# Mixing products of two transformer layers: three token tiles summed feature by feature instead of after all features

## The chip, the cores and the metric

The kernel runs on one core of a Trainium2 chip. The metric is device time in microseconds (us) of one execution, the median of three runs. Five engines are named: PE (TensorE, matrix products), DVE (VectorE), ACT (ScalarE), POOL (GpSimd) and SP (SyncE, which here issues the DMA transfers). PE writes its sums to PSUM, a memory of eight banks; one bank holds a 128x512 fp32 tile.

## What is computed

Two different transformer layers follow one another, for one sequence of T = 1024 tokens with a width of D = 1024, in fp32. The part that matters is the end of each layer's mixing stage and the step to its feed-forward part:

```python
# layer 1 (site A)
mix = jnp.concatenate([y_att, y_rwkv], axis=-1) @ w_out
x = x + g_m * rms_norm(mix, mix_post_norm)
hf = rms_norm(x, ffn_pre_norm) * (1 + sc_f) + sh_f      # then hf @ w_ffn_gate, hf @ w_ffn_up
...
# layer 2 (site B)
yb = ob @ w_b_out
mixed = jax.nn.sigmoid(gate_a) * ya + jax.nn.sigmoid(gate_b) * yb
h = h + _rmsnorm(mixed @ w_o, g_mix_post)
u2 = _rmsnorm(h, g_ffn_pre)                             # then u2 @ w_ffn_up
```

`mix` and `mixed @ w_o` are the two mixing products. Each is [1024 x 1024] times [1024 x 1024].

## The kernel before, in words

**Precision.** Every fp32 operand of these products is split into a high and a low part. One product of a pair is three matmuls (`mm3`, L101 to L107): high by high (L105), high by low (L106), low by high (L107). The split of a weight tile is an ACT copy for the high part and a subtraction on POOL or DVE for the low part (`rows_w`, L1397 and L1398); the split of a feature tile is the same in `Ops.put` (L237, L238).

**Tiles.** The tokens form 8 token tiles of 128, the 1024 features form 8 tiles k (called features below), each with its 128 rows of the weight matrix. `row_product` (L1403) computes one token tile: for each half of the 1024 output columns it sums all 8 features, 3 matmuls each, so 48 matmuls of 128x512 into one PSUM tile of two banks.

**Site A** (L1902 to L1948). The features come from DRAM: 4 to 7 first, then 0 to 3, each cast by ACT L237 and DVE L238. Weight 4 is loaded and cast early, into a free part of the feature store; the other seven are loaded on SP and cast after the last feature, in the order 5, 6, 7, 0, 1, 2, 3, the low parts shared between POOL and DVE. PSUM is laid out as two two-bank tiles `ps` for products and four one-bank tiles `tr` for transposes. Then the pipeline runs.

**The pipeline** (`pipeline`, L555, over the generator `mixed`, L1885) sends each token tile i through four steps, and in one round it issues a step each of several tiles, the newest tile first. The steps are: the product; then `stats` (ACT L534 squares and sums the PSUM tile, POOL L114 and L115 make the reciprocal root), `post_add` (DVE L542 reads the PSUM tile, DVE L543 adds the input x) and the store; then `stats` of the new x and `renorm` (DVE L549, at site A also L551); then, for two tiles together, `put_pair` (L247 to L284): eight 128x128 transposes per token tile on PE (L255) into two `tr` tiles, read by ACT (L260, L266, L272) and DVE (L261, L274 to L279), which write the operands of the feed-forward products. A `ps` tile comes free when DVE L542 has read it. Tiles `xt` and `xn` share a ring of four buffers, two token tiles' worth. Each engine works through its instructions in the order of issue.

**Site B** (L2026 to L2062). The features do not come from DRAM; each is made on PE. For m = 0 to 7, `fm` sums four inputs `ob` by `w_b_out_2` into a two-bank `ps` tile (ring of three): 24 matmuls of 128x512. DVE multiplies by a gate (L2052) and adds a tile `ma` loaded on SP (L2051, one buffer; DVE L2053); ACT L237 and DVE L238 split the result into feature m. The weights of the mixing product are loaded within the loop, m = 2 to 6, weights 0 and 1 before it and weight 7 after it, in the place of an input that `fm` no longer needs. Weight loads and `w_b_out_2` share the ring `wraw`. Then the same pipeline runs, with PSUM laid out anew as at A.

After each site the feed-forward part of the layer begins on PE (L291 to L293).

Of the kernel before, what the change touches and what calls it, by code (L numbers as in the profile page):

```python
# [19 lines left out]
D = 1024  # L20
NT = 8
# [173 lines left out]
def fm(c, w, kt, act, m0=0, m=128):  # L195

    return fms(c, [w], kt, act, m0, m)[0]


def fms(c, ws, kt, act, m0=0, m=128):  # L200

    act = Feat(act) if isinstance(act, list) else act
    ps = [c.psum([m, T]) for _ in ws]
    for hf in range(2):
        sl = slice(hf * 512, hf * 512 + 512)
        for p, w in zip(ps, ws):
            c.mm3(p[:, sl], [((w[:, 0, k, m0:m0 + m], w[:, 1, k, m0:m0 + m]), (act.cols(k, 0, hf), act.cols(k, 1, hf))) for k in range(kt)])
    return ps


def split(c, x, out_hl, eng=None):

    nc = c.nc
    nc.scalar.activation(out_hl[:, 0], x, AF.Copy)  # L214
    (eng or nc.gpsimd).tensor_sub(out_hl[:, 1], x, out_hl[:, 0].bitcast(FP))  # L215
# [315 lines left out]
def stats(c, x, junk):  # L531

    ss = c.small.tile([128, 1], FP, name="ss", tag="ssp", bufs=8)
    c.nc.scalar.activation(junk, x, AF.Square, scale=float(D) ** -0.5, accum_out=ss)  # L534
    r = c.rsqrt(ss, 1, 1.0, EPS)
    return r


def post_add(c, y, r, x, G, out, t):

    nc = c.nc
    nc.vector.scalar_tensor_tensor(t, y, r, G, op0=ALU.mult, op1=ALU.mult)  # L542
    nc.vector.tensor_add(out, t, x)  # L543


def renorm(c, t, x, r, g, b=None):

    nc = c.nc
    nc.vector.scalar_tensor_tensor(t, x, r, g, op0=ALU.mult, op1=ALU.mult)  # L549
    if b is not None:  # L550
        nc.vector.tensor_add(t, t, b)  # L551
    return t


def pipeline(gens):  # L555

    active, gens = [], iter(gens)
    more = True
    while more or active:
        g = next(gens, None)  # L560
        more = g is not None
        if more:
            active.insert(0, g)
        active = [g for g in active if next(g, active) is not active]
# [57 lines left out]
def load_rows_over(c, t, src, k, sl=slice(0, T)):  # L622

    for par in range(2):
        c.nc.sync.dma_start(t[64 * par:64 * par + 64], src[k, par, sl].partition_broadcast(64))
# [764 lines left out]
def rows_w(c, ap, w, ks, name="wo", bufs=None, at={}, eng=None):  # L1390

    nc = c.nc
    out = []
    for k in ks:
        raw = c.load_rows(w, k)
        hl = at[k] if k in at else ap.tile([128, 2, w.shape[1]], FR, name=name, bufs=bufs or len(ks) - len(at))
        nc.scalar.activation(hl[:, 0], raw, AF.Copy)  # L1397
        (eng or nc.gpsimd).tensor_sub(hl[:, 1], raw, hl[:, 0].bitcast(FP))  # L1398
        out.append(hl)
    return out  # L1400


def row_product(c, act, wt, i, ks=None):  # L1403

    ps = c.psum([128, D])
    for hf in range(2):
        sl = slice(hf * 512, hf * 512 + 512)
        c.mm3(ps[:, sl], [((act.tok(k, 0, i), act.tok(k, 1, i)), (wt[k][:, 0, sl], wt[k][:, 1, sl])) for k in ks or range(len(wt))])
    return ps
# [320 lines left out]
def row_bcast(c, ap, v, name):  # L1730

    t = ap.tile([128, D], FP, name=name)
    c.nc.sync.dma_start(t, v.partition_broadcast(128))
    return t
# [66 lines left out]
def two_layers(ctx, tc, *args):  # L1801
    out = args[-1]
    p = dict(zip(INS, args))
# [6 lines left out]
    c = Core(ctx, tc)  # L1810
    c.n8, c.n4 = 8, 6
    nc = c.nc
    pool = lambda n, side="left": tc.tile_pool(name=n, bufs=1, reuse_waits="tile", side=side)
    x1d, x2d, h1d = (tc.dram_tile([T, D], FP, name=n) for n in ("x1d", "x2d", "h1d"))
    cqd = tc.dram_tile([3, 128, 2 * T], FP, name="cqd")

    def loader(ap, src, tag="s4", bufs=None):
        def get(i):
            t = ap.tile([128, D], FP, name="xt", tag=tag, bufs=bufs or c.n4)
            nc.sync.dma_start(t, src[i * 128:(i + 1) * 128])  # L1820
            return t
        return get
# [57 lines left out]
    def store(dst, i, x):  # L1880
        nc.sync.dma_start(dst[i * 128:(i + 1) * 128], x)

    xns = [None] * NT

    def mixed(i, ap, h, wt, get, dst, G, g, b=None):  # L1885

        ps = row_product(c, h, wt, i)
        yield
        xt = get(i)
        xn = xns[i] = ap.tile([128, D], FP, name="xn", tag="s4", bufs=c.n4)  # L1890
        r = stats(c, ps, xn)
        post_add(c, ps, r, xt, G, xt, xn)
        store(dst, i, xt)
        yield
        r = stats(c, xt, xn)
        renorm(c, xn, xt, r, g, b)
        yield
        if i % 2:
            yield from h.put_pair(c, i // 2, xns[i - 1], xn)
# [5 lines left out]
    h = Ops(hp.__enter__(), "h")  # L1905
    c.layout(qk=(1, 3), tp=(1, 3), o=(1, 2))
    wt = [None] * 8
# [24 lines left out]
        features(3)  # L1932
        c.wlayout()
    at.__exit__(None, None, None)
    c.layout(ps=(2, 2), tr=(1, 4))
    wp = pool("wo1")
    wp1 = wp.__enter__()
    c.wlayout(3, 0)
    for n, k in enumerate((5, 6, 7, 0, 1, 2, 3)):
        wt[k] = rows_w(c, wp1, p["w_out"], [k], "wo", 7, eng=nc.vector if n % 3 else None)[0]  # L1940
    c.wlayout()
    c.n4 = 4
    with pool("mo2") as ap:
        g1s = h.t[:, 3, 6].rearrange("p k x t -> p (k x t)").bitcast(FP)
        nc.sync.dma_start(g1s, r1.partition_broadcast(128))
        Gh, Bh = (row_bcast(c, ap, v, n) for v, n in ((rg, "Gh"), (rb, "Bh")))
        c.tp, c.nt2 = ap, 4
        pipeline(mixed(i, ap, h, wt, loader(ap, x_in), x1d, g1s, Gh, Bh) for i in range(NT))  # L1948
    wp.__exit__(None, None, None)
    fd = tc.dram_tile([22, 128, T], FP, name="f_d")  # L1950
    c.layout(ps=(1, 8))
# [16 lines left out]
    with Down(c, pool, "d1") as dn:  # L1968
        get = loader(dn.ap, x1d)
        h = []  # L1970
# [20 lines left out]
    h = h[0]  # L1991
# [9 lines left out]
    with pool("pe") as ap:  # L2001
        pT = Tok(ap, "pT", 2)
        for i in range(NT):
            t = ap.tile([128, 256], FP, name="px", bufs=4)
            nc.sync.dma_start(t, p["p_2"][i * 128:(i + 1) * 128])
            pT.put_T(c, i, t)
        wt = rows_w(c, ap, p["w_ple_proj_2"], range(2))
        for i in range(NT):
            t = ap.tile([128, D], FP, name="et", bufs=2)
            nc.scalar.activation(t, row_product(c, pT, wt, i), AF.Copy)  # L2010
            store(ed, i, t)
# [11 lines left out]
    c.wlayout()  # L2023
    m0p.__exit__(None, None, None)
    c.wlayout(3, 4)
    c.layout(ps=(2, 3), tr=(1, 2))  # L2026
    hp = pool("hp2")
    h = Ops(hp.__enter__(), "h2")
    c.wlayout(2, 3)
# [2 lines left out]
    rows = lambda k: rows_w(c, woa, p["w_o_2"], [k], "woa", 7, eng=nc.vector if k % 2 else None)  # L2032
    wt = rows(0) + rows(1)
    with pool("mo3") as ap:
        ob = []
        for k in range(4):
            t = ap.tile([128, T], FP, name="yl", tag="ms", bufs=2)
            nc.sync.dma_start(t, obd[k])
            r = ap.tile([128, T], FP, name="yr", tag="ma", bufs=1)
            load_rows_over(c, r, b2.rd, k)  # L2040
            nc.vector.tensor_mul(t, t, r)
            y = h.free(k)
            split(c, t, y, nc.vector)
            ob.append(y)
        for m in range(8):
            ps = fm(c, c.split_w(c.load_cols(p["w_b_out_2"], m * 128, 128, 4)), 4, ob)
            if 2 <= m < 7:
                wt += rows(m)
            s, a = ap.tile([128, T], FP, name="ms", bufs=2), ap.tile([128, T], FP, name="ma", bufs=1)
            nc.sync.dma_start(s, b2.sgb[m])  # L2050
            nc.sync.dma_start(a, b2.mA[m])  # L2051
            nc.vector.tensor_mul(s, s, ps)  # L2052
            nc.vector.tensor_add(s, s, a)  # L2053
            h.put(c, m, s, nc.vector)
        wt += rows_w(c, ap, p["w_o_2"], [7], at={7: h.free(3)}, eng=nc.vector)
    c.wlayout()
    c.n4 = 4
    c.layout(ps=(2, 2), tr=(1, 4))
    with pool("mo4") as ap:
        G3, Gh = row_bcast(c, ap, p["g_mix_post_2"], "G3"), row_bcast(c, ap, p["g_ffn_pre_2"], "Gh2")  # L2060
        c.tp, c.nt2 = ap, 4
        pipeline(mixed(i, ap, h, wt, loader(ap, x2d), h1d, G3, Gh) for i in range(NT))  # L2062
    wp.__exit__(None, None, None)
    fd = tc.dram_tile([22, 128, T], FP, name="f2_d")
    c.layout(ps=(1, 8))
# [8 lines left out]
    with Down(c, pool, "d2") as dn:  # L2074
        get = loader(dn.ap, h1d)
        h = []
# [16 lines left out]
    h = h[0]  # L2093
# [5 lines left out]
    with pool("pl") as ap:  # L2099
        G5 = row_bcast(c, ap, p["g_ple_post_2"], "G5")  # L2100
        get, get_e = loader(ap, x1d), loader(ap, ed)
        wt = rows_w(c, ap, p["w_ple_gate_2"], range(8))
# [17 lines left out]
def make_kernel(fn, ins, outs, extra=None):  # L2120
    def kernel(**inputs):
# [18 lines left out]
        return got[0] if len(got)==1 else got  # L2140
    return kernel
kernel = make_kernel(two_layers, INS, [((1, 1024, 1024), "float32")], lambda: {"onehot": bucket_rows(), "inv_freq": inv_freq()})
```

## Time and profile before

| what | value |
|---|---|
| median of three runs | 3823.2 us (3817.89 to 3823.93) |
| profiled execution, its own time | 3827.49 us |
| its span, first to last instruction | 3825.8 us |
| mean granted clock of TensorE | 0.867 |
| PE busy | 3303.5 us, 86% of the span |
| DVE busy | 2363.7 us, 62% |
| ACT busy | 1422.0 us, 37% |
| POOL busy | 1086.0 us, 28% |

A row of the timeline is a start, a duration, the engine with its line and operation, the tiles out<-in, and in brackets how long the engine was idle before it and what released it. Times are us from the start of the span. PEclk is the granted clock of TensorE as a share of full speed. PE's matmuls overlap, so that two starts tell its pace and a single duration does not.

### The profile page before, as it was taken

The numbers are of one execution on the slowest core, as the hardware profiler recorded it, in microseconds if no ns is written. First come the engines' busy times: TensorE is split into PE (matmuls) and PEld (weight loads), VectorE is DVE, ScalarE is ACT, GpSimd is POOL, SyncE is SP. The second block draws the span as 40 slices with busy tenths as digits, with TensorE's granted clock in tenths as the row PEclk, the third lists the DMA queues.
The fourth block names the chain that finished last, engine by engine and source line by source line (L and its number), as shares of the span: only waits on it lengthen the run. The fifth ranks groups of instructions, "written<-read, shape, count | busy, mean of one in ns | idle before, by whom it ended". The sixth has DMA issues, their size and how long they took to land.

```text
span 3825.8 us, 42329 instructions
## 1 busy us (share of the span) xinstructions
PE 3303.5 (86%) x15652; PEld 2641.3 (69%) x15652; DVE 2363.7 (62%) x3607; ACT 1422.0 (37%) x2417; POOL 1086.0 (28%) x1007
## 2 busy tenths in 40 slices
PE   3788767998994879999897999989988799998988
PEld 2666545776773658887675888778866588886767
DVE  5569977657644365554998110016763688889983
ACT  3345433333333243333434111236642444444332
POOL 3114245424321022221444222131020122223432
PEclk7788765556566889999997999989989899999989
DMA  5462232211214122222333122210062222213234
GB/s 174 148 174 71 90 122 65 68 42 59 53 51 146 61 83 83 83 83 72 112 136 100 48 68 82 100 55 10 12 198 78 78 83 83 83 61 138 90 147 149
DMA packets 259200, 347.76 MB, mean 91 GB/s; under 512 B 17216, under 2 KB 194337, under 8 KB 257969
## 3 DMA queue, kind: packets, MB, share of 16 engines
q1 hardware_dynamic: 257936, 344.82, 27.6%
q8 instruction: 123, 2.02, 0.2%
q14 instruction: 85, 0.69, 0.1%
q0 software_dynamic: 1056, 0.23, 0.0%
HBM read 253.17 MB, written 91.83 MB: 90 GB/s over the span
## 4 chain that ended last, share of the span: by engine, by line
PE 60%; DVE 23%; DMA 7%; issue 4%; ACT 3%; POOL 2%; SPq 1%; DVEq 0%; POOLq 0%; ACTq 0%
PE ps L291 8%; PE ps L293 8%; PE ps L292 8%; PE ps L105 7%; PE ps L107 7%; PE ps L106 7%; DVE junk L845 3%; DVE sm L432 3%; DVE acc L464 2%; PE o L596 2%; DVE op L440 2%; PE tp L588 2%; DMA adaw<-in_ada_w_dram 1%; PE xy L1289 1%; DVE tmp L1225 1%
## 5 line engine op out<-in xcount | busy, mean ns | idle before, releaser
L291 PE MATMUL ps<-h,op 128*128 128x512 f32 x1232 | 481.1, 396 | 13.5 <-ACT op L314 11.6
L292 PE MATMUL ps<-h,op 128*128 128x512 f32 x1232 | 487.2, 395 | 0.0
L293 PE MATMUL ps<-h,op 128*128 128x512 f32 x1232 | 486.4, 396 | 0.0
L316 POOL TENSOR_TENSOR op<-t,op 128x512 fp32r<-128x512 f32 x88 | 129.5, 1471 | 647.8 <-ACT op L314 574.6
L291 PEld LDWEIGHTS ps<-h,op 128*128 128x128 f32 x1232 | 233.2, 189 | 69.3 <-ACT op L314 12.4
L291 PE MATMUL ps<-op,op 128*128 128x512 f32 x616 | 246.8, 403 | 34.3 <-DVE acc L464 19.7
L293 PEld LDWEIGHTS ps<-h,op 128*128 128x128 f32 x1232 | 232.7, 189 | 54.8 <-DVE op L316 0.6
L292 PEld LDWEIGHTS ps<-h,op 128*128 128x128 f32 x1232 | 232.9, 189 | 54.2
L293 PE MATMUL ps<-op,op 128*128 128x512 f32 x616 | 244.4, 397 | 6.6 <-DVE op L440 6.4
L292 PE MATMUL ps<-op,op 128*128 128x512 f32 x616 | 244.6, 397 | 6.0 <-POOL op L440 5.5
L89 POOL TENSOR_TENSOR whl<-wraw,whl 128x1024 fp32r<-128x1024 f32 (+1 forms) x62 | 130.2, 2102 | 392.2 <-ACT whl L88 363.4
L1710 DVE TENSOR_TENSOR up<-t,ps 128x512 f32<-128x512 f32 x176 | 116.6, 683 | 199.4 <-ACT t L354 153.7
L354 ACT ACTIVATE t<-ps 128x512 f32<-128x512 f32 x132 | 78.5, 595 | 384.1 <-PE ps L293 382.1
L105 PE MATMUL ps<-h,whl 128*128 128x512 f32 x512 | 205.8, 404 | 9.6 <-ACT h L214 7.9
L107 PE MATMUL ps<-h,whl 128*128 128x512 f32 x512 | 204.9, 400 | 1.2 <-POOL whl L89 1.2
L106 PE MATMUL ps<-h,whl 128*128 128x512 f32 x512 | 205.3, 401 | 0.3 <-DVE h L215 0.3
L464 DVE TENSOR_TENSOR acc<-acc,ps 128x1024 f32<-128x1024 f32 x152 | 180.1, 1208 | 10.1 <-PE ps L293 9.0
L596 PE MATMUL o<-pT,v 128*128 128x256 f32 (+1 forms) x640 | 157.9, 366 | 13.4 <-ACT pT L591 7.8
L291 PEld LDWEIGHTS ps<-op,op 128*128 128x128 f32 x616 | 117.5, 191 | 74.1 <-DVE acc L464 18.4
L591 ACT ACTIVATE pT<-tp 128x512 fp32r<-128x512 f32 (+2 forms) x221 | 94.6, 444 | 186.9 <-PE tp L588 149.4
L114 POOL TENSOR_SCALAR rs_y<-ss 128x1 f32<-128x1 f32 (+2 forms) x90 | 32.7, 364 | 457.0 <-ACT xn L534 283.0
L438 ACT ACTIVATE op<-sm 128x1024 fp32r<-128x1024 f32 (+1 forms) x96 | 94.5, 987 | 177.0 <-DVE sm L432 149.5
(589 smaller groups left out, 8342.7 us busy)
## 6 DMA issues: line engine op xcount, KB each, us to landing
wraw<-in_w_ffn_up_dram SPq DMA_DIRECT2D x66, 512.0 KB, 4.0
adaw<-in_ada_w_dram SPq DMA_DIRECT2D x96, 256.0 KB, 3.5
raw<-in_w_ffn_down_dram SPq DMA_DIRECT2D x44, 512.0 KB, 6.5
raw<-f_d SPq DMA_DIRECT2D x44, 512.0 KB, 5.3
wraw<-in_w_in_dram SPq DMA_DIRECT2D x42, 512.0 KB, 3.9
wraw<-in_w_ffn_gate_dram SPq DMA_DIRECT2D x22, 512.0 KB, 3.9
f_d<-up SPq DMA_DIRECT2D x22, 512.0 KB, 2.6
f_d<-cv SPq DMA_DIRECT2D x22, 512.0 KB, 2.6
```

What stands on the lines that cost most here:

```text
L89: self.nc.gpsimd.tensor_sub(hl[:, 1], raw, hl[:, 0].bitcast(FP))
L105: self.nc.tensor.matmul(out, lh, rh, start=first and i == 0, stop=False)
L106: self.nc.tensor.matmul(out, lh, rl, start=False, stop=False)
L107: self.nc.tensor.matmul(out, ll, rh, start=False, stop=last and i == n - 1)
L291: mm(out, lh, rh, start=start and i == 0, stop=False, skip_group_check=True)
L292: mm(out, lh, rl, start=False, stop=False, skip_group_check=True)
L293: mm(out, ll, rh, start=False, stop=stop and i == n - 1, skip_group_check=True)
L316: (nc.gpsimd if n[0] % 7 in (0, 3, 5) else nc.vector).tensor_sub(t[:, 1], x, t[:, 0].bitcast(FP))
L432: getattr(eng, what)(x, a, b)
L464: nc.vector.tensor_add(d, d, ps[q])
L596: nc.tensor.matmul(o[:, q], v[:, b0 + s].rearrange("p a d -> p (a d)"), pT[:, x, s, q], start=b0 == 0 and n == 0, stop=end and n == 3)
L1710: nc.vector.tensor_add(halves(x[j])[e], tok(a), tok(b))
```

## The change

There are three parts.

First, a new function `k_step` adds one feature's part to three PSUM tiles: 3 token tiles x 2 halves x 3 matmuls, so 18. It is called for each feature as soon as feature and weight are issued. The three PSUM tiles hold token tiles 0 to 2; their step of the product falls away from `mixed`, and these tiles enter the pipeline with their statistics. Tiles 3 to 7 are computed by `row_product` as before. PSUM is laid out for both as three two-bank tiles `po` and two one-bank tiles `tr`.

Second, at site A weight 4's step comes first, the low parts of the seven other weights all go to DVE, and each weight's step follows its cast.

Third, at site B a feature is made in two halves of 512 columns, each in a one-bank `tr` tile, since the two-bank tiles are taken; the gate is multiplied by half (two instructions in place of one). The step of feature m - 1 stands behind the making of feature m. The layout is not changed between the loop and the pipeline.

```diff
+def k_step(c, act, w, k, pss, first, last):
+
+    for i, ps in enumerate(pss):
+        for hf in range(2):
+            sl = slice(hf * 512, hf * 512 + 512)
+            c.mm3(ps[:, sl], [((act.tok(k, 0, i), act.tok(k, 1, i)), (w[:, 0, sl], w[:, 1, sl]))], first, last)
...
-def row_product(c, act, wt, i, ks=None):
+def row_product(c, act, wt, i, ks=None, tag="ps"):
-    ps = c.psum([128, D])
+    ps = c.psum([128, D], tag)
...
-    def mixed(i, ap, h, wt, get, dst, G, g, b=None):
-        ps = row_product(c, h, wt, i)
-        yield
+    def mixed(i, ap, h, wt, pss, get, dst, G, g, b=None):
+        if i < len(pss):
+            ps = pss[i]
+        else:
+            ps = row_product(c, h, wt, i, tag="po")
+            yield
...
-    c.layout(ps=(2, 2), tr=(1, 4))
+    c.layout(po=(2, 3), tr=(1, 2))
+    pss = [c.psum([128, D], "po") for _ in range(3)]
...
-    for n, k in enumerate((5, 6, 7, 0, 1, 2, 3)):
-        wt[k] = rows_w(c, wp1, p["w_out"], [k], "wo", 7, eng=nc.vector if n % 3 else None)[0]
+    for n, k in enumerate((4, 5, 6, 7, 0, 1, 2, 3)):
+        if n:
+            wt[k] = rows_w(c, wp1, p["w_out"], [k], "wo", 7, eng=nc.vector)[0]
+        k_step(c, h, wt[k], k, pss, n == 0, n == 7)
...
-    c.layout(ps=(2, 3), tr=(1, 2))
+    c.layout(po=(2, 3), tr=(1, 2))
...
+        pss = [c.psum([128, D], "po") for _ in range(3)]
         for m in range(8):
-            ps = fm(c, c.split_w(c.load_cols(p["w_b_out_2"], m * 128, 128, 4)), 4, ob)
-            if 2 <= m < 7:
-                wt += rows(m)
+            w = c.split_w(c.load_cols(p["w_b_out_2"], m * 128, 128, 4))
             s, a = ap.tile([128, T], FP, name="ms", bufs=2), ap.tile([128, T], FP, name="ma", bufs=1)
             nc.sync.dma_start(s, b2.sgb[m])
             nc.sync.dma_start(a, b2.mA[m])
-            nc.vector.tensor_mul(s, s, ps)
+            for hf in range(2):
+                sl = slice(hf * 512, hf * 512 + 512)
+                ps = c.psum([128, 512], "tr")
+                c.mm3(ps, [((w[:, 0, k], w[:, 1, k]), (ob[k][:, 0, sl], ob[k][:, 1, sl])) for k in range(4)])
+                nc.vector.tensor_mul(s[:, sl], s[:, sl], ps)
+            if 2 <= m < 7:
+                wt += rows(m)
+            if m:
+                k_step(c, h, wt[m - 1], m - 1, pss, m == 1, False)
             nc.vector.tensor_add(s, s, a)
             h.put(c, m, s, nc.vector)
         wt += rows_w(c, ap, p["w_o_2"], [7], at={7: h.free(3)}, eng=nc.vector)
+        k_step(c, h, wt[7], 7, pss, False, True)
...
-    c.layout(ps=(2, 2), tr=(1, 4))
```

The gate's multiplication is L2069 after the change (L2052 before), the addition of `ma` L2074 (L2053 before).

The order of the instructions moves with it. Three places follow.

The first is PE at the end of site A: the last matmuls of token tile 7's product, then transposes (L255), then the feed-forward part. Before:

```order
L106 MATMUL ps<-wo,h 128x512
L107 MATMUL ps<-wo,h 128x512
L105 MATMUL ps<-wo,h 128x512
L106 MATMUL ps<-wo,h 128x512
L107 MATMUL ps<-wo,h 128x512
L255 MATMUL tr<-ident,xn 128x128 x32
L291 MATMUL ps<-h,op 128x512
```

With the change:

```order
L106 MATMUL po<-wo,h 128x512
L107 MATMUL po<-wo,h 128x512
L105 MATMUL po<-wo,h 128x512
L106 MATMUL po<-wo,h 128x512
L107 MATMUL po<-wo,h 128x512
L255 MATMUL tr<-ident,xn 128x128 x40
L291 MATMUL ps<-h,op 128x512
```

Before, the transposes of four token tiles stand behind the last product; now those of five do. In both, the transposes ahead of these stand behind tile 6's product.

The second is ACT at site A, from the last weight cast on. L534 on `ps` or `po` is the reader of a product, L534 on `xt` the second statistics, L266 and L260 read a transpose tile. Before:

```order
L1397 ACTIVATE wo<-wraw 128x1024 x7
L534 ACTIVATE xn,ss<-ps 128x1024 x2
L534 ACTIVATE xn,ss<-xt 128x1024
L266 ACTIVATE t_9625<-tr 128x512
L260 ACTIVATE h<-tr 128x4x128
L534 ACTIVATE xn,ss<-ps 128x1024
L534 ACTIVATE xn,ss<-xt 128x1024
L266 ACTIVATE t_9634<-tr 128x512
L260 ACTIVATE h<-tr 128x4x128
L272 ACTIVATE t_9710<-tr 128x512
```

With the change:

```order
L1397 ACTIVATE wo<-wraw 128x1024 x7
L534 ACTIVATE xn,ss<-po 128x1024 x2
L534 ACTIVATE xn,ss<-xt 128x1024
L266 ACTIVATE t_9565<-tr 128x512
L260 ACTIVATE h<-tr 128x4x128
L534 ACTIVATE xn,ss<-po 128x1024
L534 ACTIVATE xn,ss<-xt 128x1024
L266 ACTIVATE t_9574<-tr 128x512
L260 ACTIVATE h<-tr 128x4x128
L534 ACTIVATE xn,ss<-xt 128x1024
L534 ACTIVATE xn,ss<-po 128x1024
```

The third product is read behind the first transposes in both. The fourth is now read ahead of the second token tile's transposes (L272) and not behind them.

The third is DVE at site B: L2052 or L2069 is the gate, L2053 or L2074 the addition of `ma`, L238 the low part of a feature, L1398 that of a weight. Before:

```order
L2052 TENSOR_TENSOR ms<-ms,ps 128x1024
L2053 TENSOR_TENSOR ms<-ms,ma 128x1024
L2052 TENSOR_TENSOR ms<-ms,ps 128x1024
L238 TENSOR_TENSOR h_20188<-ms,h_20188 128x4x2x128
L2053 TENSOR_TENSOR ms<-ms,ma 128x1024
L2052 TENSOR_TENSOR ms<-ms,ps 128x1024
L238 TENSOR_TENSOR h_20188<-ms,h_20188 128x4x2x128
L2053 TENSOR_TENSOR ms<-ms,ma 128x1024
L238 TENSOR_TENSOR h_20188<-ms,h_20188 128x4x2x128
L2052 TENSOR_TENSOR ms<-ms,ps 128x1024
L1398 TENSOR_TENSOR woa<-wraw,woa 128x1024
```

With the change:

```order
L2069 TENSOR_TENSOR ms<-ms,tr 128x512 x2
L2074 TENSOR_TENSOR ms<-ms,ma 128x1024
L238 TENSOR_TENSOR h_20188<-ms,h_20188 128x4x2x128
L2069 TENSOR_TENSOR ms<-ms,tr 128x512 x2
L2074 TENSOR_TENSOR ms<-ms,ma 128x1024
L238 TENSOR_TENSOR h_20188<-ms,h_20188 128x4x2x128
L2069 TENSOR_TENSOR ms<-ms,tr 128x512
L1398 TENSOR_TENSOR woa<-wraw,woa 128x1024
L2069 TENSOR_TENSOR ms<-ms,tr 128x512
```

Each gate is two instructions of 512 columns, and a feature's low part now stands ahead of the next feature's gate, where before the gate came first for some.

## Rows read from the trace of the kernel before

**Rows 1.** The page, the chain that ended last, by engine.

```profile
PE 60%; DVE 23%; DMA 7%; issue 4%; ACT 3%; POOL 2%; SPq 1%; DVEq 0%; POOLq 0%; ACTq 0%
```

**Rows 2.** Timeline of PE at A: start us, us, operation, count [idle before, releaser].

```profile
1219.62 1.22 PE L105 MATMUL ps<-wo,h 128*128 128x512 f32 x2 [41.62 <-ACT wo L1397]
```

**Rows 3.** Timeline of ACT at A: casts of features (L237) and weights (L1397).

```profile
1207.81 1.06 ACT L237 ACTIVATE h<-yl 128x1024 fp32r<-128x1024 f32 x1 [3.51 <-DVE yl L1917]
1210.16 2.95 ACT L1397 ACTIVATE wo<-wraw 128x1024 fp32r<-128x1024 f32 x3 [1.29 <-DVE h L238]
...
1225.77 1.06 ACT L1397 ACTIVATE wo<-wraw 128x1024 fp32r<-128x1024 f32 x1 [3.64 <-DMA wraw<-in_w_out_dram]
```

**Rows 4.** Timeline of PE at A: first and last of six like matmuls, 24 apart.

```profile
1238.54 0.39 PE L105 MATMUL ps<-h 128*128 128x512 f32 x1
...
1265.74 0.39 PE L105 MATMUL ps<-h 128*128 128x512 f32 x1
```

**Rows 5.** Timeline of PE at A, after a stop: first and last of ten matmuls.

```profile
1274.55 0.63 PE L107 MATMUL ps<-wo,h 128*128 128x512 f32 x1
...
1278.39 0.63 PE L107 MATMUL ps<-wo,h 128*128 128x512 f32 x1
```

**Rows 6.** Windows at A: length, busy (count) of PE, PEld, DVE, ACT, POOL, PEclk, DMA, GB/s.

```profile
1230.00:1270.00 40.00, 39.50 (x179) 32.56 (x177) 7.25 (x6) 4.10 (x8) 2.25 (x6) 1.00 0.14 51
1270.00:1343.00 73.00, 56.87 (x224) 45.84 (x224) 32.92 (x38) 18.46 (x36) 7.24 (x16) 0.86 0.16 58
```

**Rows 7.** Timeline of A, one stop between tiles, PE, ACT and DVE.

```profile
1268.47 1.03 PE L255 MATMUL tr<-ident,xn 128*128 128x128 f32 x8
1269.16 0.60 ACT L266 ACTIVATE t<-tr 128x512 f32<-128x512 f32 x1 [20.11 <-PE tr L255]
...
1270.13 1.03 ACT L534 ACTIVATE xn<-ps 128x1024 f32<-128x1024 f32 x1
...
1272.19 1.28 DVE L542 SCALAR_TENSOR_TENSOR xn<-ps,rs_y,h 128x1024 f32<-128x1024 f32 x1 [1.22 <-POOL rs_y L115]
...
1273.53 0.80 PE L105 MATMUL ps<-wo,h 128*128 128x512 f32 x1 [4.03 <-DVE xn L542]
```

**Rows 8.** Timeline of A, tail: transposes on PE, one L551 on DVE.

```profile
1322.79 1.03 PE L255 MATMUL tr<-ident,xn 128*128 128x128 f32 x8
...
1333.84 1.22 DVE L551 TENSOR_TENSOR xn<-xn,Bh 128x1024 f32<-128x1024 f32 x1
...
1341.88 1.03 PE L255 MATMUL tr<-ident,xn 128*128 128x128 f32 x8
...
1375.15 0.79 PE L291 MATMUL ps<-h,op 128*128 128x512 f32 x1 [5.79 <-ACT op L314]
```

**Rows 9.** Timeline of PE at B, with one L549 on DVE.

```profile
2823.13 1.22 PE L105 MATMUL ps<-h,whl 128*128 128x512 f32 x2 [3.12 <-ACT h L214]
...
2868.14 0.50 PE L105 MATMUL ps<-woa,h 128*128 128x512 f32 x1 [2.40 <-DVE ms L2052]
...
2876.87 0.79 PE L105 MATMUL ps<-h 128*128 128x512 f32 x1 [2.55 <-ACT h L237]
...
2916.27 1.04 PE L255 MATMUL tr<-ident,xn 128*128 128x128 f32 x8
...
2970.63 1.03 PE L255 MATMUL tr<-ident,xn 128*128 128x128 f32 x8
...
2976.88 1.27 DVE L549 SCALAR_TENSOR_TENSOR xn<-xt,rs_y,Gh 128x1024 f32<-128x1024 f32 x1
...
2988.46 1.04 PE L255 MATMUL tr<-ident,xn 128*128 128x128 f32 x8
...
3016.41 0.80 PE L291 MATMUL ps<-h,op 128*128 128x512 f32 x1 [5.77 <-ACT op L314]
```

**Rows 10.** The tile ma at B: its adds on DVE, the time of its loads.

```profile
L2053 DVE TENSOR_TENSOR ms<-ms,ma x8: 1215/1516/2618, 2831.4 to 2874.5; 128x1024 f32<-128x1024 f32 x8
...
DMA to landing us min/median/max: 3.4/4.3/5.0
```

More of the change, by code (lines that the diff above doesn't have):

```diff
@@ L1947, in two_layers @@
         c.tp, c.nt2 = ap, 4
-        pipeline(mixed(i, ap, h, wt, loader(ap, x_in), x1d, g1s, Gh, Bh) for i in range(NT))
+        pipeline(mixed(i, ap, h, wt, pss, loader(ap, x_in), x1d, g1s, Gh, Bh) for i in range(NT))
     wp.__exit__(None, None, None)
@@ L2061, in two_layers @@
         c.tp, c.nt2 = ap, 4
-        pipeline(mixed(i, ap, h, wt, loader(ap, x2d), h1d, G3, Gh) for i in range(NT))
+        pipeline(mixed(i, ap, h, wt, pss, loader(ap, x2d), h1d, G3, Gh) for i in range(NT))
     wp.__exit__(None, None, None)
```

## Prediction

> **What bounds the kernel now.** I read the chain of waits first: TensorE carries 60% of it and VectorE 23% [rows 1], so a gain has to come from time in which TensorE stands still or runs slowly. The diff touches two places: the mixing product of layer 1 (site A) and of layer 2 (site B). At A, TensorE idles 41.62 us until a weight is ready at 1219.62 [rows 2]. The inputs are there long before: the last feature is cast at 1207.81, three weights are cast from 1210.16, the last one at 1225.77 [rows 3]. Nothing is done with them, because the first tile wants all eight.
>
> Then the clock. Six rows of one repeating matmul, 24 matmuls apart, go from 1238.54 to 1265.74: 27.2/120 = 0.2267 us each, or 10.88 per token tile of 48 [rows 4]. Just after a stop it is (1278.39 - 1274.55)/9 = 0.427 [rows 5]. [...]
>
> Those stops: tile 3's transposes start at 1268.47, ScalarE copies their output (L266) at 1269.16, and only behind that copy squares tile 2's sums (L534, 1270.13), though tile 2 was done 11 us before. VectorE reads the sums at 1272.19, the PSUM buffer comes free, and tile 4 starts at 1273.53 [rows 7]. (The transposes are token tile 0's, but stand behind product 3.) From there to the transposes behind tile 7 (1341.88) four tiles take 73.41 us [rows 7, 8]. Unbroken they would take 4 x (10.88 + 1.03); so one stop costs (73.41 - 47.64)/4 = **6.44 us**, the wait and the half-clock matmuls after it together. At B: (2988.46 - 2916.27 - 47.64)/4 = **6.14** [rows 9].
>
> The tail is a chain of VectorE, ScalarE and transposes: 1341.88 to the first matmul of the feed-forward part at 1375.15, 33.27 us [rows 8]; at B 2988.46 to 3016.41, 27.95 [rows 9].
>
> **Site A, step by step.** The 384 matmuls remain; 144 of them (tiles 0 to 2) go into three PSUM tiles, 18 per weight. Weight 4 is cast before the wait, so its 18 fall into the idle 41.62 us: no cost. The next 18 start after the first cast of the run of three (a third of 2.95 behind 1210.16, 1211.1). After a long idle they run at 0.427: 7.7 us. The other 108 take 24.5 at 0.2267, to 1243.3. No weight is late: the last, cast at 1225.77 plus 1.06, is used from 1239.2. The three remainders move from POOL to VectorE, idle there; a wait of one such subtraction (1.2 us, L1398 on VectorE) is the bound.
>
> Before, tile 2 ended at 1268.47 - 10.88 = 1257.6 [rows 7]: **head start 14 us**. Tile 3 needs tile 0's buffer. Tile 0's last six matmuls end 12 matmuls (2.7) before 1243.3, L542 starts 2.06 after L534 and takes 1.28 [rows 7]: free at about 1244.0, a wait of 0.7. Then tile 3 to 1255.0; tiles 4 and 5 with a transpose group each (11.91 each) to 1278.8; tile 6 to 1289.7. Here the third buffer works: L542 of tile 2 still stands behind token tile 0's transposes, at about 1259, but tile 5 wants that buffer only at 1267. The order on PE puts the third transpose group behind tile 6, and tile 7 wants tile 4's buffer, whose L534 stands behind it: one stop. Tile 7 ends at 1289.7 + 1.03 + 10.88 + 6.44 = 1308.1. Four stops have become one, **3 x 6.44 = 19.3**.
>
> It is given back in part: the PE order ends with 40 transposes behind tile 7 where it had 32, so the tail has one token tile more. From the fourth group (1322.79) to the end of L551 for the next tile (1333.84 + 1.22) were 12.27 us [rows 8]. So: 1308.1 + 12.27 + 33.27, and 1 us for transposes at half clock and two transpose buffers in place of four (bounds 0 and 3: four groups at most, each waiting one 0.7-us read), is 1354.6 in place of 1375.15. **A: -20.5.**
>
> **Site B.** Per feature m, 24 matmuls make the feature and 18 add the one before: 42 x 0.2267 = 9.52 us. Before, the pace was VectorE's: eight L2053 from 2831.4 to 2874.5, one per 6.16 us, held by the single buffer of loads that land in 3.4 to 5.0 us [rows 10]. TensorE now sets the pace, and these loads have 3.4 us of slack. At 2823.13 [rows 9], when the last input feature is there, 318 of the 192 + 144 matmuls remain (the 18 of feature 0's first three inputs are done; two one-bank buffers let no more start): 72.1 us, 3.4 for the first 7 us at half clock, 0.9 once for a wait on those buffers: 2899.5. Tile 0's last weight part waits about 1 us on VectorE's queue (now behind L1398), the kind of wait that took 2.55 at 2876.87 [rows 9]; tile 3 starts at 2900.7. Splitting L2052 in two halves costs VectorE 0.2 us per feature, hidden by the 9.52. Then, as at A, 10.88 + 2 x 11.91 + 10.88 + (11.91 + 6.14): tile 7 ends at 2964.3. Tail: 2976.88 + 1.27 - 2970.63 = 7.52 [rows 9], 27.95 and 1: 3000.8 for 3016.41, -15.6. SP issues two weight loads ahead of the feature's own; with 4 us of room I take 0.6 for it (bounds 0 and 3, one load). **B: -15.**
>
> **Sum:** -35.5. The profiled execution (3827.5, span 3825.8 and 1.7 around it; 4.3 above the median 3823.2) would be 3792; on the median's scale **3788**.
>
> [...] After a gap of 2.40 us the first matmul of a run lasts 0.50 us; after 2.55 it lasts 0.79, as after the 4.03 of a stop (0.80) [rows 7, 9]. [...]
>
> **Rivals.**
> (1) *TensorE stops in every feature of B.* A feature's matmuls need the one-bank buffers read by L2069, which stands on VectorE behind the last feature's L2053, which waits for a load. If TensorE waits there as long as at 2876.87 or longer, each feature costs a stop: 8 x 6.14 = 49, total +13.6: **3837**, slower. It decides where the load chain grows from 6.16 us to over 12; for it, these loads set the pace even now [rows 10]; against it, the 3.4 us of room. Chance 0.04.
> (2) *The third buffer does not cover.* If VectorE's and ScalarE's queues put L542 later than I worked out, stops return. Room at A is 1267 - 1260.5 = 6 us. All three back at both sites: -35.5 + 19.3 + 18.4 = +2, **3825**; half of them: 3807. Chance 0.14, half of it inside 0.2%.
> (3) *The longer tail is hidden.* If the fifth group's chain runs while TensorE still multiplies, 12.3 + 7.5 come back: -55, **3768**. Against it, the 40 transposes at the end in the order. Chance 0.08.
> (4) *The early sums are not early*, as the new PSUM layout waits for the attention's buffers: weight 4's 18 matmuls move to 1211, 4 to 8 us: 3794, inside the forecast's range.
> (5) *Every step waits*, at A for weights and at B for features, so that the 7 steps of A and the 8 features of B run at half clock throughout: 7 x 18 x 0.2 + 8 x 42 x 0.2 = 92 us on the forecast, **3880**. Chance 0.02.
>
> **How the numbers follow.** Forecast (3778 to 3806, gains of 17 to 45, which takes in both ends of the small bounds, one stop more at each site, and half of the tail) 0.72; rivals (1) 0.04, (2) 0.14, (3) 0.08, (5) 0.02. The likeliest is 3788. With 0.2% being 7.6 us, about what a measurement can tell: faster 0.72 + 0.08 + 0.07 = 0.87, same 0.07, slower 0.06.
>
> **What would show it.** In the changed profile: 18 po matmuls before 1211 at A and no idle over 2 us from 1211 to 1289; one wait on L542 per site, ahead of tile 7, in place of four; the feed-forward part's first matmul 20 us earlier at A and 35 at B; at B features 9.5 us apart at a granted clock near 1.00. Four waits left, a clock under 0.9 between 2830 and 2895, or a tail over 50 us after tile 7 would make it wrong.

## The result, and the profile after

The changed kernel takes 3782.61 us (median of three runs, 3782.47 to 3786.22) against 3823.2: a ratio of 0.9901 with a 95% interval of 0.9878 to 0.9923, so 40.6 us faster. The forecast was 3788 in a range of 3778 to 3806. Measured a second time beside before's runs on the same chip the ratio was 0.9904 (0.9884 to 0.9925).

The profiled execution took 3782.61 us, its span is 3780.9, its mean granted clock 0.874 (0.867 before).

The timeline of PE at site A after the change answers to [rows 2, 7, 8]: the end of the attention (L596), the early step, the first matmul behind the casts, tile 3's first, the transposes and the one long wait, the last group, the tail, the feed-forward part.

```profile
1165.99 0.80 PE L596 MATMUL o<-pT,v 128*128 128x128 f32 x2 [0.59 <-DVE pT L592]
1168.94 0.80 PE L105 MATMUL po<-h 128*128 128x512 f32 x1 [2.16 <-ACT h L237]
...
1202.58 1.65 PE L105 MATMUL po<-wo,h 128*128 128x512 f32 x3 [27.42 <-ACT wo L1397]
...
1234.00 0.50 PE L105 MATMUL po<-wo,h 128*128 128x512 f32 x1 [0.73 <-DVE xn L542]
...
1245.47 1.03 PE L255 MATMUL tr<-ident,xn 128*128 128x128 f32 x8
...
1258.83 1.03 PE L255 MATMUL tr<-ident,xn 128*128 128x128 f32 x8
...
1279.46 1.04 PE L255 MATMUL tr<-ident,xn 128*128 128x128 f32 x8
1284.53 0.50 PE L105 MATMUL po<-wo,h 128*128 128x512 f32 x1 [4.03 <-DVE xn L542]
...
1297.16 1.03 PE L255 MATMUL tr<-ident,xn 128*128 128x128 f32 x8
...
1309.51 1.94 PE L255 MATMUL tr<-ident,xn 128*128 128x128 f32 x8 [11.31 <-DVE xn L551]
...
1343.81 0.80 PE L291 MATMUL ps<-h,op 128*128 128x512 f32 x1 [5.79 <-ACT op L314]
```

The idle time is still there, 27.42 us, but weight 4's 18 matmuls lie ahead of it, and tiles 0 to 2 follow at once. Tile 3 waits 0.73 us for a buffer (0.7 was worked out). From there one wait of 4.03 us is left where there were four, ahead of tile 7, and a fifth token tile's transposes stand in the tail: 11.31 us to 1309.51.

That wait has the same chain as before [rows 7], on ACT, DVE and PE (timeline of the change, us from the start):

```profile
1280.16 0.60 ACT L266 ACTIVATE t<-tr 128x512 f32<-128x512 f32 x1 [13.74 <-PE tr L255]
...
1281.13 1.03 ACT L534 ACTIVATE xn<-po 128x1024 f32<-128x1024 f32 x1
...
1283.19 1.28 DVE L542 SCALAR_TENSOR_TENSOR xn<-po,rs_y,h 128x1024 f32<-128x1024 f32 x1 [1.22 <-POOL rs_y L115]
```

Site B, PE, for [rows 9]: the first matmul of feature 2 and that of feature 7, tile 3's, tile 7's, the transposes behind it, the feed-forward part.

```profile
2805.23 0.40 PE L105 MATMUL tr<-h,whl 128*128 128x512 f32 x1
...
2853.66 0.40 PE L105 MATMUL tr<-h,whl 128*128 128x512 f32 x1
...
2869.25 0.50 PE L105 MATMUL po<-woa,h 128*128 128x512 f32 x1 [1.67 <-DVE xn L542]
...
2919.84 0.64 PE L105 MATMUL po<-woa,h 128*128 128x512 f32 x1 [4.03 <-DVE xn L542]
...
2932.45 1.03 PE L255 MATMUL tr<-ident,xn 128*128 128x128 f32 x8
...
2968.68 0.79 PE L291 MATMUL ps<-h,op 128*128 128x512 f32 x1 [5.78 <-ACT op L314]
```

Five features take 2853.66 - 2805.23 = 48.43 us, 9.69 each (9.52 was worked out).

The windows of the change (length, busy us and count of PE, PEld, DVE, ACT, POOL, then the granted clock, DMA share, GB/s): the products of A, its tail, the features of B, its products.

```profile
1243.00:1297.00 54.00, 49.97 (x226) 41.24 (x225) 22.59 (x25) 14.09 (x26) 4.44 (x12) 0.97 0.16 59
1297.00:1343.00 46.00, 8.98 (x42) 7.13 (x40) 35.43 (x44) 21.30 (x40) 7.85 (x14) 0.56 0.34 103
2800.00:2868.00 68.00, 67.58 (x294) 54.93 (x292) 32.87 (x30) 15.99 (x19) 14.19 (x8) 1.00 0.47 157
2868.00:2933.00 65.00, 59.72 (x270) 49.32 (x271) 24.94 (x27) 15.12 (x28) 5.92 (x16) 0.97 0.22 85
```

The granted clock holds 1.00 through the features of B, and is 0.97 through A's products from the first transposes on, where it was 0.86 [rows 6].

### The profile page after: what moved, and what is told of

Same layout as the page of the kernel before. It is cut to its first block, busy times and chain, and to the rows that moved or that the text cites. A ratio compares the mean times of both kernels' runs of the same rounds, so it can differ in the third digit from the quotient of the medians.

```text
span 3780.9 us, 42331 instructions
## 1 busy us (share of the span) xinstructions
PE 3273.3 (87%) x15652; PEld 2615.8 (69%) x15652; DVE 2371.2 (63%) x3618; ACT 1421.3 (38%) x2417; POOL 1078.9 (29%) x1004
## 4 chain that ended last, share of the span: by engine, by line
PE 60%; DVE 24%; DMA 7%; issue 4%; ACT 3%; POOL 2%; SPq 1%; DVEq 0%; POOLq 0%; ACTq 0%
PE ps L291 8%; PE ps L292 8%; PE ps L293 8%; PE ps L107 5%; PE ps L105 5%; PE ps L106 5%; DVE junk L845 4%; DVE sm L432 3%; DVE acc L464 2%; DVE op L440 2%; PE o L596 2%; PE tp L588 2%; PE po L105 2%; PE po L106 2%; PE po L107 1%
## 5 line engine op out<-in xcount | busy, mean ns | idle before, releaser
L291 PE MATMUL ps<-h,op 128*128 128x512 f32 x1232 | 482.6, 397 | 13.5 <-ACT op L314 11.6
L291 PEld LDWEIGHTS ps<-h,op 128*128 128x128 f32 x1232 | 232.9, 189 | 70.3 <-ACT op L314 12.4
L291 PE MATMUL ps<-op,op 128*128 128x512 f32 x616 | 247.6, 404 | 38.8 <-DVE acc L464 22.5
L105 PE MATMUL ps<-h,whl 128*128 128x512 f32 x448 | 177.7, 397 | 1.6 <-ACT whl L88 1.6
L106 PE MATMUL ps<-h,whl 128*128 128x512 f32 x448 | 177.5, 396 | 0.0
L107 PE MATMUL ps<-h,whl 128*128 128x512 f32 x448 | 177.1, 396 | 0.3 <-POOL whl L89 0.3
L291 PEld LDWEIGHTS ps<-op,op 128*128 128x128 f32 x616 | 118.0, 192 | 79.3 <-ACT op L438 24.9
L596 PE MATMUL o<-pT,v 128*128 128x256 f32 (+1 forms) x640 | 156.5, 362 | 15.3 <-ACT pT L591 9.6
```

The costliest lines, as they stand in the source:

```text
L105: self.nc.tensor.matmul(out, lh, rh, start=first and i == 0, stop=False)
L106: self.nc.tensor.matmul(out, lh, rl, start=False, stop=False)
L107: self.nc.tensor.matmul(out, ll, rh, start=False, stop=last and i == n - 1)
L291: mm(out, lh, rh, start=start and i == 0, stop=False, skip_group_check=True)
L596: nc.tensor.matmul(o[:, q], v[:, b0 + s].rearrange("p a d -> p (a d)"), pT[:, x, s, q], start=b0 == 0 and n == 0, stop=end and n == 3)
```

## What the experiments compare

In every profile site A is taken from the end of the attention's last L596 to the first L291 of the feed-forward part, and site B likewise in layer 2; all times in us. In before that is 1375.15 - 1178.00 = 197.15 and 3016.41 - 2805.29 = 211.12. A stop is a wait of 3.4 us or more for L542; waits for L543 are not in that column, and in f2, f3 and f5 one of 3.4 to 5.1 us stands at each site. The tail runs from the last product's end.

| kernel | site A | site B | stops A, B | tail A, B | time, ratio to before |
|---|---|---|---|---|---|
| before | 197.2 | 211.1 | 4, 4 | 33.1, 27.8 | 1 |
| before, once more (e0) | 197.5 | 208.1 | 4, 4 | 33.1, 27.8 | one run |
| the change | 177.0 | 195.7 | 1, 1 | 46.5, 36.1 | 0.9901 (0.9878 to 0.9923) |
| the change, once more (e6) | 177.0 | 195.4 | 1, 1 | 46.5, 36.1 | 0.9904 (0.9884 to 0.9925) |
| only A (e1) | 177.0 | 208.8 | 1, 4 | 46.5, 27.8 | 0.9955 (0.9939 to 0.9970) |
| only B (e2) | 197.6 | 195.1 | 4, 1 | 33.1, 36.1 | 0.9973 (0.9956 to 0.9989) |
| three buffers alone (e3) | 201.7 | 209.2 | 3, 3 | 46.5, 36.1 | 0.9997 (0.9976 to 1.0018) |
| two tiles early, two buffers (e4) | 182.0 | 199.9 | 3, 3 | 33.1, 27.8 | 0.9924 (0.9899 to 0.9948) |
| one bank for features (e5) | 177.3 | 221.8 | 1, 1 | 46.5, 44.0 | one run |
| low parts on POOL (f1) | 180.2 | 199.2 | 1, 1 | 49.4, 39.7 | 0.9915 (0.9901 to 0.9928) |
| the change, xn not needed (f2) | 164.3 | 191.3 | 0, 0 | 38.0, 33.4 | 0.9855 (0.9838 to 0.9872) |
| f1 and f2 together (f3) | 164.9 | 192.0 | 0, 0 | 38.7, 34.9 | 0.9880 (0.9865 to 0.9895) |
| before, xn not needed (f4) | 174.3 | 184.7 | 0, 0 | 36.3, 29.7 | 0.9876 (0.9855 to 0.9897) |
| e4, xn not needed (f5) | 169.2 | 183.6 | 0, 0 | 36.3, 29.7 | 0.9867 (0.9847 to 0.9887) |

## The experiments

**Is it the sites? Before again (e0), the change again (e6).** No edit.

> The kernel before, unchanged, profiled once more, to see how much a stretch that the change does not touch varies from one execution to the next. In the two profiles so far the stretch from the start to the attention's last matmul of layer 1 took 1178.0 us before and 1166.8 after, 11.2 less, with the same instructions in the same order. Theory V (variation): this profile puts that matmul anywhere between 1165 and 1180, and site A (from there to the feed-forward part's first matmul) again at 197 us within 2, site B at 211 within 2. Rival U (the change makes the stretch ahead of it faster): this profile shows 1178 within 2 again.

> The whole change once more, to size the stretches that it does not touch. Theory V: sites at 177 and 196 us within 1, the stretch ahead of site A anywhere between 1155 and 1180 us, so that the 5 us by which the measured gain exceeded the sites' 35.5 are chance. Rival U: the stretch ahead of A is again near 1167, ten less than before's 1177 to 1178.

The stretch ahead of site A took 1177.0 us in e0. In e6, the last L596 stands at

```profile
1179.34 0.80 PE L596 MATMUL o<-pT,v 128*128 128x128 f32 x2 [0.58 <-DVE pT L592]
```

so 1180.1, against 1166.8 in the first profile of the same kernel. The same instructions in the same order thus differ by 13 us between two executions, and over all fourteen profiles the stretch runs from 1155.2 (e4) to 1180.4 (f3). Rival U falls. Site A repeats to 0.5 us; site B of before does not repeat to the 2 us that I had put (211.1, 208.1, and 208.8 in e1).

**One site at a time (e1, e2).**

```diff
# e1: site B's lines, its layouts and its pipeline as before
# e2: site A's lines, its layout and its pipeline as before
-        pipeline(mixed(i, ap, h, wt, pss, loader(...), ...) for i in range(NT))
+        pipeline(mixed(i, ap, h, wt, (), loader(...), ...) for i in range(NT))
```

> Site A changed, site B as before. By the prediction's terms site A takes 20 us less (177 in place of 197, as in the profile of the whole change), site B stays at 211 within 2, and the time falls by 20 (ratio 0.995). Rival, one site's gain depends on the other (the clock or the queues carry over): site A's gain differs by more than 4 us from the whole change's. Rival U: the stretch ahead of A is shorter by 10 as well, and the time falls by 30.

> Site B changed, site A as before. By the prediction's terms site B takes 15 us less (196 in place of 211), site A stays at 197 within 2, the time falls by 15 (ratio 0.996). Rival U: as the stretch ahead of A has nothing changed behind it before site B, it says nothing; rival of carry-over: site B's gain differs by more than 4 us from 15.

Site A gains 20.1 whether B is changed or not, and site B 14 to 16, whether A is. Nothing carries over from site to site. The ratios are those of about 17 and 10 us, together 10 us or more short of the whole change's 38 to 41; with intervals of some 6 us each way for either run, the run times neither show nor exclude that the two add. The sites' own times do add.

**The third buffer alone (e3).**

```diff
-    c.layout(ps=(2, 2), tr=(1, 4))
+    c.layout(ps=(2, 3), tr=(1, 2))      # both sites, the kernel before otherwise
```

> The kernel before with three product buffers and two transpose buffers at both sites, and no early sums: the third buffer by itself. In its order the transposes stand one product later, 40 of them behind the last. My theory: the third buffer is worth something only together with the early tiles. With every product in a row the tile that wants a buffer still waits for statistics behind the transposes, three stops in place of four, and the tail is one token tile longer: at A -6.4 + 13.3 = +7, at B -6.1 + 8.5 = +2, so 9 slower in all (ratio 1.002). Rival, the buffer removes the stops whatever else happens (one stop left): A -19.3 + 13.3 = -6, B -18.4 + 8.5 = -10, so 16 faster.

Site A is 4.6 us longer and site B within its scatter; the ratio's interval holds 1. Three stops are left at each site, as the first theory had it (timeline of PE at A: the three stops, the first transposes behind the last product, then those that wait for L551):

```profile
1281.42 0.50 PE L105 MATMUL ps<-wo,h 128*128 128x512 f32 x1 [4.03 <-DVE xn L542]
...
1299.26 0.50 PE L105 MATMUL ps<-wo,h 128*128 128x512 f32 x1 [4.15 <-DVE xn L542]
...
1316.90 0.80 PE L105 MATMUL ps<-wo,h 128*128 128x512 f32 x1 [3.97 <-DVE xn L542]
...
1329.44 1.03 PE L255 MATMUL tr<-ident,xn 128*128 128x128 f32 x8
...
1341.84 1.94 PE L255 MATMUL tr<-ident,xn 128*128 128x128 f32 x8 [11.37 <-DVE xn L551]
```

So the third buffer alone takes away one stop, and the longer tail (46.5 for 33.1) takes back more.

**The early sums with two buffers (e4).**

```diff
-    c.layout(po=(2, 3), tr=(1, 2))
-    pss = [c.psum([128, D], "po") for _ in range(3)]
+    c.layout(po=(2, 2), tr=(1, 4))
+    pss = [c.psum([128, D], "po") for _ in range(2)]    # both sites
```

> The change with early sums for two token tiles only, two product buffers and four transpose buffers: the head start without the third buffer. Its order of transposes is that of before (32 behind the last product). By the prediction's terms site A has a head start of some 12 us (two tiles end at 1232.6 + a wait of 2 in place of 1246.8), the four stops and the old tail stay: 185 us in place of 197. Site B: 36 matmuls per feature, 185 of its 211 us are not touched, head start 6 less a wait of 2: 207. Both together -16 (ratio 0.996). Rival, the head start is all there is to it and the buffer adds nothing: the same times as the whole change, 177 and 196. Other rival, the buffer is all: 197 and 211.

Both sites do better than I worked out, 15 and 8 to 11 us less than in the profiles of before where 12 and 4 were expected, since one of the four stops goes here too (PE at A: tile 2's first matmul and the three stops):

```profile
1214.66 0.50 PE L105 MATMUL po<-wo,h 128*128 128x512 f32 x1 [2.09 <-DVE xn L542]
...
1255.25 0.77 PE L105 MATMUL po<-wo,h 128*128 128x512 f32 x1 [4.24 <-DVE xn L542]
...
1273.62 0.55 PE L105 MATMUL po<-wo,h 128*128 128x512 f32 x1 [3.97 <-DVE xn L542]
...
1291.57 0.77 PE L105 MATMUL po<-wo,h 128*128 128x512 f32 x1 [4.30 <-DVE xn L542]
```

The early sums of two tiles, with the old tail, thus give most of the whole change's gain at the sites; the third buffer and the third tile add 5.0 at A and 4.1 at B (the table's rows).

**The tail's queue (f1).**

```diff
# in put_pair, of the change
-        put(self.S1, s1, nc.vector)
+        put(self.S1, s1, nc.gpsimd)     # and so S2, S3, S4
```

> The whole change, with the low parts of four of the seven transposed operands (made from tiles that are not in PSUM) on POOL in place of VectorE. If the longer tail is a queue on VectorE, as I take it to be, the two groups in the tail in which such subtractions stand ahead of L551 or L549 of the next tile (four of 0.6 us each) become 2.4 us shorter each: tails of 42 and 31 us in place of 46.5 and 36.1, and some 9 us less than the whole change in all. Rival, the tail is a chain of waits (transposes, copies, statistics) in which VectorE is seldom the last: tails unchanged within 1 us.

Neither: the tails became 3 to 4 us longer. VectorE has fewer instructions ahead of L551, but L543 and L551 last longer where four L261 on POOL, 7.35 us in all, run beside them. The timeline of f1 in the tail of A:

```profile
1299.27 7.35 POOL L261 TENSOR_TENSOR h<-t,h 128x512 fp32r<-128x512 f32 x4
...
1301.01 0.68 DVE L261 TENSOR_TENSOR h<-tr,h 128x512 fp32r<-128x512 f32 x1
...
1303.22 2.28 DVE L543 TENSOR_TENSOR xt<-xn,xt 128x1024 f32<-128x1024 f32 x1
...
1305.42 2.28 DVE L551 TENSOR_TENSOR xn<-xn,Bh 128x1024 f32<-128x1024 f32 x1
```

and the same place in the change:

```profile
1302.81 0.68 DVE L261 TENSOR_TENSOR h<-tr,h 128x512 fp32r<-128x512 f32 x1
...
1305.20 1.22 DVE L543 TENSOR_TENSOR xt<-xn,xt 128x1024 f32<-128x1024 f32 x1
...
1308.15 1.22 DVE L551 TENSOR_TENSOR xn<-xn,Bh 128x1024 f32<-128x1024 f32 x1
```

L543 and L551, both with two inputs in SBUF, take 2.28 us in place of 1.22, while L261 on a transpose tile, one of its inputs in PSUM, takes 0.68 in both.

**What a product's reader waits for (f2, and f3 with f1).**

```diff
# in mixed
-        r = stats(c, ps, xn)
-        post_add(c, ps, r, xt, G, xt, xn)
+        junk = h.t[:, 2, 6].rearrange("p k x t -> p (k x t)") if i < 6 else xn
+        r = stats(c, ps, junk)
+        post_add(c, ps, r, xt, G, xt, ps)
...
-        r = stats(c, xt, xn)
+        r = stats(c, xt, junk)
```

The squares themselves are used by nobody, only their sum is, so they can go to any free place; the product is scaled where it lies. L542 no longer writes to `xn`, nor does L534 for token tiles 0 to 5, and L543 is now the last to read the product's buffer.

> The whole change, with the squares of the statistics written to a free part of the feature store (token tiles 0 to 5) and the first step of post_add written over the product in PSUM, so that a product's reader does not need the buffer xn that the transposes of two tiles earlier still read. In its order on ScalarE the reader of tile 4's product stands ahead of token tile 2's transposes. Theory: the one stop left at each site comes from that buffer and that order; it goes, and the sites take 6.4 and 6.1 us less (171 and 190). Rival: the stop goes but VectorE's and ScalarE's chain sets the end of the site anyway, and the tail grows by as much: 177 and 196.

> The last two together. If stop and tail are separate terms, the gains add: 166 and 185 us at the sites, some 21 us less than the whole change (ratio to before 0.984). If the chain sets the end, it brings no more than the larger of the two.

The stop goes at both sites. Site A gains 12.7 us, twice what was expected: its tail is shorter too (38.0 for 46.5), and some 2 us lie ahead of the first weight, which the edit does not touch. Site B gains 4.1 to 4.5 where 6.1 was expected. The tail does not give the stop back, but part of it comes back at tile 3, which now waits for L543: 3.37 us at A where it was 0.73, and 4.04 at B where it was 1.67 (timeline of PE, A and B):

```profile
1242.40 0.73 PE L105 MATMUL po<-wo,h 128*128 128x512 f32 x1 [3.37 <-DVE xt L543]
...
2869.95 0.47 PE L105 MATMUL po<-woa,h 128*128 128x512 f32 x1 [4.04 <-DVE xt L543]
```

In f2 the second group behind the last product no longer waits for L551; it starts 0.25 us behind the first, and its second half waits for a transpose buffer (timeline of PE, A):

```profile
1301.23 1.04 PE L255 MATMUL tr<-ident,xn 128*128 128x128 f32 x8
1302.53 0.66 PE L255 MATMUL tr<-ident,xn 128*128 128x128 f32 x4 [0.25 <-ACT t L272]
1307.72 1.08 PE L255 MATMUL tr<-ident,xn 128*128 128x128 f32 x4 [4.54 <-DVE h L261]
1314.78 1.94 PE L255 MATMUL tr<-ident,xn 128*128 128x128 f32 x8 [5.97 <-DVE xn L551]
```

f3 is no faster than f2: the expected sum fell with f1's half of it.

**The same edit without the change (f4), and with two early tiles (f5).** The edit of f2 in the kernel before, and in e4.

> The kernel before (no early sums, two product buffers), with only the statistics' squares in the feature store and post_add over the product in PSUM. If a product's reader waits for the buffer xn that the transposes of two tiles earlier hold, and not for a lack of product buffers, then two product buffers are enough: no stop at either site. Its order ends with 40 transposes, which cost f2 a tail of 38.0 and 33.4 us: site A 197 - 4 x 6.44 + 5 = 176, site B 211 - 4 x 6.14 + 5.6 = 192, in all as fast as the whole change (ratio 0.990). Rival, the product buffers are what lacks: the four stops stay and the tail makes it slower, 202 and 217.

> Early sums for two token tiles, two product buffers, with the statistics' squares in the feature store. If head start and stops are separate terms, it takes from the two-tile kernel (182 and 200 us) three stops and adds the longer tail: 182 - 19.3 + 5 = 168, 200 - 18.4 + 5.6 = 187; in all within 4 us of f2's 164.3 and 191.3. Rival, without the third buffer stops return: 175 or more at A.

With two product buffers and no early sums there is no stop left. The windows of f4, products of A and of B:

```profile
1230.00:1311.00 81.00, 81.00 (x373) 67.29 (x372) 34.41 (x35) 19.74 (x36) 9.90 (x22) 1.00 0.19 72
2850.00:2937.00 87.00, 85.82 (x394) 71.02 (x393) 31.20 (x33) 20.87 (x38) 9.88 (x22) 1.00 0.24 87
```

TensorE is busy 81.00 of 81.00 us. So it is not product buffers that were lacking. Nor do the transposes standing one product later explain it by themselves: 40 of them stand behind the last product in e3 too, and e3 has three stops at each site. f4's sites sum to 359.0 us, less than the whole change's 372.8; in the run times the two intervals still overlap. f5 lies at 352.8 and f2 at 355.5; their ratios don't separate them. In f5 a wait of 4.73 us comes back at A ahead of tile 2, for L543, since the buffer is now freed one instruction later, and one of 5.07 at B. With these waits in them the early sums of two tiles are worth 5.1 at A and 1.0 at B (f4 to f5), the latter inside the 3 us by which site B varies. At B two tiles do better than three (183.6 for 191.3); 3.7 of that is the tail, the rest was not taken apart.

**Waits between features (e5).**

```diff
# site B only
-    c.layout(po=(2, 3), tr=(1, 2))
+    c.layout(po=(2, 3), tr=(1, 1), fm=(1, 1))
...
-                ps = c.psum([128, 512], "tr")
+                ps = c.psum([128, 512], "fm")
```

> The whole change, but site B's features are made in a single one-bank buffer (and the transposes there have one, too), so that TensorE must wait within every feature for VectorE's half gate. My reading of the rows of before: a wait of about 1.2 us (0.7 for the gate, the rest for the two hand-overs) does not cost the clock; eight of them add 10 us, the features come 10.9 us apart in place of 9.7, at a granted clock near 1.00 from feature 1 on. [...]

PE waits once in every feature, for 0.78 us ahead of its first half, and the granted clock stays at 1.00 (timeline of PE, the start of features 2 and 3; window of the features):

```profile
2816.21 0.50 PE L105 MATMUL fm<-h,whl 128*128 128x512 f32 x1 [0.78 <-DVE ms L2069]
...
2826.99 0.50 PE L105 MATMUL fm<-h,whl 128*128 128x512 f32 x1 [0.78 <-DVE ms L2069]
```

```profile
2808.00:2878.00 70.00, 65.32 (x277) 51.29 (x276) 25.24 (x27) 12.07 (x13) 14.19 (x6) 1.00 0.43 147
```

The features come 2826.99 - 2816.21 = 10.78 us apart (10.9 was expected), at a granted clock of 1.00. Of the 26 us by which site B is longer than the change's, 16 lie ahead of tile 3: 5.5 between features 2 and 7, the others in the loop's start and behind its end, where TensorE waits 3.13 us for feature 7's cast. The products take 2 more and the tail, with one bank for the transposes, 8. The run has waits of 0.78 us in every 10.78; what longer waits in every feature would have done was not tried.

## Why the prediction was right, and where it was not

**The sum.** Forecast -20.5 at A and -15 at B. Measured, over the profiles in which a site was changed or not: A 197.4 (before, e0, e2) to 177.0 (the change, e1, e6), -20.4; B 209.3 (before, e0, e1) to 195.4 (the change, e2, e6), -13.9. That is 34.3 of the 40.6 us by which the medians differ. The other 6 were found in no place that the change touches; the stretch ahead of A alone varies by more than that, and the second measurement of the change gave 38 us between the medians.

At B the changed site came out as worked out (196.1 worked out, 195.4 measured); the forecast gain is 1 us too large since it was taken from 211.1, the longest of the three profiles with B unchanged.

**Step by step, A.** The half clock in the sums is what the windows of before have behind a stop: 0.50 from 1274.50 to 1278.50, where the matmuls of [rows 5] lie, against 1.00 in the unbroken stretch [rows 6]. The idle time before the change was read wrongly in one point: TensorE does not wait until the first tile has all eight weights. That tile's sum begins with weight 0, the fourth to be cast behind 5, 6 and 7, and TensorE starts at 1219.62, when that cast ends (timeline of ACT, before):

```profile
1218.52 1.06 ACT L1397 ACTIVATE wo<-wraw 128x1024 fp32r<-128x1024 f32 x1 [5.41 <-DMA wraw<-in_w_out_dram]
```

What it would bring to begin each sum with weights 4 to 7, without early sums, was not tried; it is a rival for a part of the head start. An estimate of its worth: the last weight's low part is ready at 1229.3 in before and tile 0 ends near 1268.47 - 3 x 10.88 = 1235.8, so at most some 6 of the 14 us. With the change, weight 4's step lies in the idle time: as put. The second step began 1.1 us behind the cast (1.0 worked out; timeline of ACT, the change):

```profile
1201.48 2.95 ACT L1397 ACTIVATE wo<-wraw 128x1024 fp32r<-128x1024 f32 x3 [1.29 <-DVE h L238]
```

From it to tile 3 the change took 1234.00 - 1202.58 = 31.4 us, 32.9 worked out. From tile 3 to the transposes behind the last product 1297.16 - 1234.00 = 63.2 (64.1 worked out), the tail 46.5 (46.5). That the site agrees so closely is luck in part: these two stretches are 2.4 us shorter than worked out, and the weights' first cast comes 34.7 us behind the attention's end where 32.2 was taken over from before. That distance runs from 32.2 to 35.3 over the fourteen profiles.

**Step by step, B.** Features every 9.69 us for 9.52, the loads out of the way: VectorE waited for the loads of the `ma` tile 0.6 us in all, in 2 waits, where it was 8.5 us in 5 before (the tile `ma`, before and change):

```profile
  DMA ma<-mA_d: 8.5, 5
...
  DMA ma<-mA_d: 0.6, 2
```

Tile 3 waited 1.67 us on L542, the end of weight 7's step being on time. One stop, and a tail of 36.1 for 36.5.

**The rivals.** Stops in every feature (1, 5): none in the change; in e5 TensorE waits 0.78 us in each feature, and the window over the features has a granted clock of 1.00, as in the change, not half clock throughout. The third buffer not covering (2): it covers in the change, but e3 shows it doesn't by itself. The longer tail hidden (3): no, the tails are 13.4 and 8.3 us longer, and the table shows with what: e3, the third buffer alone, has the long tails, e4, the early sums with two buffers, the old ones. The early sums late (4): no.

**What the prediction had wrong** is the reason of one term. "Here the third buffer works", it said, and gave the buffer three stops. e3 and e4 take that apart: alone, buffer and early sums each remove one stop of four, and only together three. And the stop itself was read one step short. L534 stands behind L266 on ScalarE [rows 7]; I took that for the order and looked for room in PSUM. The reader stood there because L534 and L542 wrote to `xn`, whose buffer the transposes of two token tiles earlier still read. f4 shows it: with that need gone, two product buffers and no early sums, no stop is left. Both writes were moved together; which of the two alone would have held the reader back was not tried. The ring of four for `xt` and `xn` was in the text on the kernel, and was not in the sum.

## What to carry to other kernels

A wait for a buffer has two questions: which buffer the waiting engine names, and what keeps that buffer's reader from reading; here two scratch outputs, the squares and the scaled product, held the reader back, and moving them was worth as much as the whole change (0.9876 for 0.9901, intervals overlapping). A part of a change can give back what another part gains: at A the terms were 14 us of head start and 19 of stops, and 13 went back into a longer tail that came with the third buffer. Measure a part of a long kernel from anchor to anchor in the profile: the stretch ahead of site A varies by 25 us between executions, the two sites by 0.5 and 3.

## What the runs showed of the hardware

Beside the four subtractions on POOL in the tail of A in f1, L543 and L551 on VectorE, each with two inputs in SBUF, took 2.28 us where the change took 1.22; that was not expected, and f1, expected to gain 9 us, lost about 7 at the sites. With a wait of 0.78 us in each feature of 10.78 the granted clock was 1.00 in e5; at A of before, with four stops, waits of 3.97 to 4.30, it was 0.86 from 1270 to 1343 [rows 6]. In before the length of the first matmul after a wait did not tell the clock of those behind it: after 2.55 us it was 0.79 and after 4.03 us 0.80 [rows 7, 9], but after 4.24 us 0.47, with 0.63 from the third on, and the granted clock behind was 0.50 all three times (2877 to 2879, 1274.50 to 1278.50, 1293.15 to 1296.10; timeline of PE at A, before):

```profile
1292.60 0.47 PE L105 MATMUL ps<-wo,h 128*128 128x512 f32 x1 [4.24 <-DVE xn L542]
...
1293.15 0.63 PE L107 MATMUL ps<-wo,h 128*128 128x512 f32 x1
```
